# Moving GpSimd's barrier wait from behind the closing semaphore clear to ahead of it, in a row-sum kernel

## The chip, the cores and the metric

The kernel runs on one core of one Trainium2 chip. The metric is device time in microseconds; a kernel's time is the median of its executions. "The span" is the time from the first to the last recorded instruction of one profiled execution; the time holds some 1.78 us more than the span of the same execution (1.78 in both profiled kernels and all runs below but one). Engines are called VectorE (DVE), ScalarE (ACT), GpSimd (POOL), TensorE (PE) and SyncE (SP); a q behind such a name, as in POOLq or PEldq (TensorE), marks what the engine's sequencer runs itself. A transfer's landing is an update of its semaphore by the DMA; the last store has 16 of them, from 159.665 to 159.834 us in the kernel before, and counts as landed with the 16th (the clear that waits for it starts 24 ns later). The closing is the name here for what the trace holds behind the span's end: in the kernel before, 18 updates of one semaphore from 235 to 1902 ns behind it, and one or two of each of 246 others; the texts put it down to the runtime, which no trace shows. A wait is called met when its condition already holds as the engine comes to it.

## The reference

```python
def reference(x):            # x: 32 x 512 x 1024 float32
    return np.sum(x, axis=-1).astype(np.float32)
```

## The kernel before

The body streams x into SBUF in blocks of 16 rows per partition and sums rows on VectorE, with ScalarE helping at the end. It ends with a last store of 8 KB from SyncE. Behind the body stands a closing block that the framework writes: SyncE waits for what is outstanding, a first barrier of all engines, GpSimd's clear of the range of semaphores that the program used, and a second barrier. In a barrier the four other engines each run a drain that adds 1 to a "gather" semaphore, and then wait for a "release" semaphore; GpSimd waits until gather holds 4, takes 4 off, and adds 4 to release. An earlier change, already in the kernel before, lets the clear itself, not SyncE, wait for the landing of the last store:

```python
def wait_for_the_store_at_the_clear(nc):
    end = nc.main_func.blocks[-1]
    insts = list(end.instructions)
    # ... finds SyncE's last store and SyncE's drain ahead of the first barrier ...
    (wait,) = [w for w in info.on_wait if w.ant_name == stored]
    rest = [w for w in info.on_wait if w.ant_name != stored]
    insts[at] = copy.replace(
        insts[at], sync_info=mybir.SyncInfo(on_wait=rest, on_update=info.on_update)
    )
    clear = next(
        k
        for k, i in enumerate(insts)
        if i.engine == mybir.EngineType.Pool and isinstance(i, mybir.InstISA)
    )
    # ...
    insts[clear] = copy.replace(
        insts[clear], sync_info=mybir.SyncInfo(on_wait=[wait], on_update=[])
    )
    end.instructions = insts
```

As built, GpSimd's part of the closing block is, in order (gather and release stand for the barrier's two semaphores):

```
drain
wait gather >= 4, gather -= 4      first barrier
release += 4
drain
clear of the program's semaphores  waits for the last store's landing
drain
wait gather >= 4, gather -= 4      second barrier
release += 4
```

## Time and profile before

| | before |
|---|---|
| time, median of 3 (lowest to highest) | 161.72 us (161.71 to 161.91) |
| span of the profiled execution | 160.24 us, time of that execution 162.02 |
| DMA, mean over the span | 419 GB/s, 67.18 MB |
| last landing of the last store to the clear | 24 ns |
| clear's start to the span's end | 383 ns |

The first three rows say where the time goes: into the stream (the chain that ended last is DMA for 73% and VectorE for 25% of the span). The last two are what the change can touch. They come from the trace's records of single instructions and of semaphore updates, since the views round to 0.1 us. The lines of the views themselves are shown in the prediction. One further view of the kernel before, the DMA issues by line with KB each and us from issue to landing, shows the store that the clear waits for:

```profile
out_dram<-sums ACTq DMA_DIRECT2D x1, 56.0 KB, 2.1
out_dram<-sums SPq DMA_DIRECT2D x1, 8.0 KB, 1.4
```

The second line is the last store: 1.4 us from its issue at 158.41 us to its landing at 159.83, and inside those 1.4 us the first barrier ends (its last arrival is counted at 159.14) and all four arrivals of the second come in (the last at 159.46).

### The profile page before, as it was taken

What the parts mean: (1) busy time and instruction counts of PE and PEld (TensorE: products, weight loads), DVE (VectorE), ACT (ScalarE), POOL (GpSimd) and SP (SyncE); (2) the same over time, 40 slices, a digit from 0 to 9 for tenths busy, and PEclk for the clock granted to TensorE, in tenths of its full rate; (3) what the DMA queues carried; (4) which work ended last, traced back from release to release, by engine and by line L of the source; (5) the groups of instructions that cost most, each with busy time, mean ns of one, the idle gap of its engine ahead of it and who ended that gap; (6) DMA issues with size and microseconds to landing.
All of it is one profiled execution on the core that took longest, in us unless ns stands there. A gap on an engine that the chain in (4) does not pass through costs nothing.

```text
span 160.2 us, 125 instructions
## 1 busy us (share of the span) xinstructions
DVE 120.1 (75%) x22; ACT 17.3 (11%) x31; POOL 0.2 (0%) x4
## 2 busy tenths in 40 slices
DVE  0190059960799959999499994999949999497953
ACT  3000000000000000000000000000000000496953
POOL 0000000000000000000000000000000000000000
DMA  7999996996996996989969969969969969899994
GB/s 270 450 479 503 393 524 262 523 523 262 524 523 262 523 524 262 523 360 425 524 262 523 523 262 524 523 262 523 523 262 523 507 278 523 376 409 410 424 382 109
DMA packets 2928, 67.18 MB, mean 419 GB/s; under 512 B 1264, under 2 KB 1392, under 8 KB 1520
## 3 DMA queue, kind: packets, MB, share of 16 engines
q1 hardware_dynamic: 2016, 67.12, 97.7%
q10 hardware_dynamic: 912, 0.06, 0.3%
HBM read 67.11 MB, written 0.07 MB: 419 GB/s over the span
## 4 chain that ended last, share of the span: by engine, by line
DMA 73%; DVE 25%; SPq 1%; issue 0%; DVEq 0%
DMA t<-in_x_dram 73%; DVE sums L131 24%; SPq L170 1%; SPq L211 0%; DVE t L145 0%; DVEq L242 0%
## 5 line engine op out<-in xcount | busy, mean ns | idle before, releaser
L131 DVE TENSOR_REDUCE sums<-t 128x16 f32<-128x16384 f32 (+3 forms) x9 | 116.6, 12953 | 35.9 <-DMA t<-in_x_dram 35.9
L158 ACT ACTIVATE unread<-t 128x1024 f32<-128x1024 f32 x15 | 15.2, 1012 | 139.7 <-DMA t<-in_x_dram 139.7
L145 DVE CUSTOM_DVE_ANT_0 t<-t 128x512 f32<-128x512 f32 (+2 forms) x6 | 3.5, 602 | 2.4 <-DMA t<-in_x_dram 2.3
L158 ACT ACTIVATION_READ_ACCUMULATOR unread<-t 128x1 f32 x15 | 2.8, 187 | 0.0
L158 ACT ACT_TABLE_LOAD x1 | 1.3, 1283 | 0.8 <-PEq L231 0.8
L145 DVE DVE_READ_ACCUMULATOR2_ANT sums<- 128x1 f32 x5 | 0.4, 83 | 0.0
L231 POOL MEMSET const-bfloat16-1.0<- 128x1 bf16 x1 | 0.1, 101 | 0.0
L231 POOL MEMSET const-uint8-127<- 128x1 uint8 x1 | 0.1, 101 | 0.0
L231 POOL MEMSET const-float32-0.0<- 128x1 f32 x1 | 0.1, 98 | 0.2 <-issue 0.2
L231 POOL MEMSET const-float32-1.0<- 128x1 f32 x1 | 0.1, 98 | 0.0
L145 DVE DVE_READ_ACCUMULATOR2_ANT t<- 128x1 f32 x1 | 0.1, 83 | 0.0
L209 DVE MEMSET t<- 128x1 f32 x1 | 0.1, 59 | 0.0
## 6 DMA issues: line engine op xcount, KB each, us to landing
t<-in_x_dram SPq DMA_DIRECT2D x1, 6144.0 KB, 21.0
t<-in_x_dram SPq DMA_DIRECT2D x1, 4096.0 KB, 31.2
t<-in_x_dram SPq DMA_DIRECT2D x1, 2560.0 KB, 37.0
t<-in_x_dram SPq DMA_DIRECT2D x1, 2048.0 KB, 7.2
t<-in_x_dram SPq DMA_DIRECT2D x1, 1024.0 KB, 39.0
t<-in_x_dram SPq DMA_DIRECT2D x1, 280.0 KB, 39.2
t<-in_x_dram SPq DMA_DIRECT2D x1, 232.0 KB, 39.3
t<-in_x_dram SPq DMA_DIRECT2D x6, 41.1
```

The source lines that it names most:

```text
L131: return nc.vector.tensor_reduce(out=dst, in_=src, axis=mybir.AxisListType.X, op=mybir.AluOpType.add)
L145: return nc.vector.tensor_tensor_reduce(out=src[:, :n], in0=src[:, :n], in1=src[:, n:], scale=1.0, scalar=0.0, op0=mybir.AluOpType.add, op ...
L158: nc.scalar.activation(out=unread[:, :n], in_=src, func=mybir.ActivationFunctionType.Copy, accum_out=dst,)
L170: load = nc.sync.dma_start(out=block, in_=rows_from(j, n))
L209: nc.vector.memset(whole[:, width + 1 :], 0.0)
L231: nc = _bacc.Bacc("TRN2", target_bir_lowering=False, num_devices=1)
```

## The change

GpSimd's wait for the other engines at the second barrier goes ahead of the clear. It then falls into the time in which GpSimd waits for the store to land anyway (in the trace before, 369 ns from the last arrival at 159.465 to the landing at 159.834), and behind the clear only a drain stands ahead of the release. Nothing is added or dropped.

```diff
     insts[clear] = copy.replace(
         insts[clear], sync_info=mybir.SyncInfo(on_wait=[wait], on_update=[])
     )
+
+
+    at = next(
+        k
+        for k in range(clear + 1, len(insts))
+        if insts[k].engine == mybir.EngineType.Pool and isinstance(insts[k], mybir.InstEventSemaphore)
+    )
+    assert insts[at].sync_info.on_wait and "gather" in insts[at].sync_info.on_wait[0].ant_name
+    met = insts.pop(at)
+    insts.insert(clear, met)
     end.instructions = insts
```

## The prediction

From the recorded texts (this one and the expectation of after_again) passages are cut that told of the hardware what no run of this case shows; the cuts are marked. The sum here: one step of 79 ns off the span, 160.241 - 0.079 = 160.162 us, and with the 1.48 us outside the span 161.64 us. What the time outside the span consists of was not shown. "Here it is" stands for the part of the store's time behind its last packet, and "these" in rival B for the updates of the closing. That the cleared range does not hold the barrier's two semaphores shows in the trace before: those updated 21 to 65 ns behind the clear's start are 99 to 108, the barrier's are 96 and 97.

> **What bounds the kernel now.** I read the page first, part 1 and part 2, to see whether the change can touch what the kernel spends its time on.
>
> ```profile
> span 160.2 us, 125 instructions
> DVE 120.1 (75%) x22; ACT 17.3 (11%) x31; POOL 0.2 (0%) x4
> ...
> DMA  7999996996996996989969969969969969899994
> GB/s 270 450 479 503 393 524 262 523 523 262 524 523 262 523 524 262 523 360 425 524 262 523 523 262 524 523 262 523 523 262 523 507 278 523 376 409 410 424 382 109
> ```
>
> The DMA row stands at 6 to 9 tenths in every slice but the first and the last: the kernel is a stream of 67.11 MB from HBM, and VectorE (75% busy) follows it. GpSimd has 0.2 us of work in all. So the change is not in the stream. I then asked for busy time by stretches.
>
> ```profile
> core 0: us, DVE busy (x) ACT busy (x) POOL busy (x), PEclk, DMA share, GB/s
> 120.00:150.00 30.00, 26.80 (x3) 10.41 (x19) 0.00 (x0) 1.00 0.99 428
> 150.00:158.40 8.40, 5.94 (x14) 5.61 (x12) 0.00 (x0) 1.00 0.89 350
> 158.40:160.20 1.80, 0.00 (x0) 0.00 (x0) 0.00 (x0) 1.00 0.05 5
> ```
>
> The last row is the stage that the change edits: 1.80 us in which no engine does counted work and the DMA share is 0.05. It is 1.1% of the span. Even if the whole of it vanished the time would fall by less than 2%. The chain that ended last stops short of it, at the last sum:
>
> ```profile
> 24 pieces in order of time: start us, us, what
> ...
> 118.59 39.34 DMA t<-in_x_dram
> 157.93 0.05 issue
> 157.97 0.40 DVE t L145
> 158.38 0.01 DVEq L242
> ```
>
> So I went to the closing block itself: the view of the instructions that stand at the launch's line, limited to the window from 159.3 to 160.3 us.
>
> ```profile
> L242 ACTq EVENT_SEMAPHORE  x2: 17/17/17, 159.3 to 160.2; - x2
> L242 DVEq EVENT_SEMAPHORE  x2: 21/21/21, 159.3 to 160.2; - x2
> L242 PEldq EVENT_SEMAPHORE  x2: 51/51/51, 159.3 to 160.2; - x2
> L242 POOLq DRAIN  x2: 34/52/70, 159.3 to 160.0; - x2
> L242 POOLq EVENT_SEMAPHORE  x2: 17/17/17, 160.1 to 160.1; - x2
> ...
> L242 POOLq EVENT_SEMAPHORE_RANGE_CLEAR  x1: 93/93/93, 159.9 to 159.9; - x1
> ```
>
> Both semaphore instructions of GpSimd in this window stand behind the clear, at 160.1 us; the other engines are released at 160.2. One of the two is the wait that the change moves. The page rounds to 0.1 us, so the sizes below come from the trace's own records, in ns from the span's start, for the same instructions:
>
> ```
> 158412  SP store of the last 8 KB issued (348)
> 159240  first barrier: GpSimd's release
> 159321  GpSimd drain (70)
> 159373  SP, 159378 ACT, 159402 DVE, 159444 PE: drains of the second barrier
> 159465  last of the four arrivals counted on the gather semaphore
> 159464  last packet of the store ends
> 159834  16th landing of the store counted on its semaphore
> 159858  GpSimd clear of the semaphore range (93)
> 159980  GpSimd drain (34)
> 160058  GpSimd wait for the four arrivals (17)
> 160137  GpSimd release (17)
> 160178  SP, 160183 ACT, 160189 DVE, 160190 PE (51): released
> 160241  end of the span (PE's release instruction ends)
> ```
>
> The tail is one chain: store issue, landing at 159.834, clear 24 ns later, drain, gather wait, release, and the four releases. The four other engines had arrived at 159.465, some 370 ns before the store landed and almost 600 ns before GpSimd looks for them. The gather wait at 160.058 therefore waits for nothing; it costs only its own step.
>
> [...] the gather's record is 17 ns long, but the next instruction of GpSimd starts 79 ns after it (160058 to 160137), and the same pair in the first barrier is 78 ns apart (159162 to 159240). So 79 and not 17 ns is the cost of the step. [...] Here it is the 370 ns from the last packet's end (159464) to the last landing (159834): that wait is what the moved instruction can hide in.
>
> **The change part by part.** The diff takes GpSimd's wait for the gather semaphore (at least 4, then minus 4) from behind the drain that follows the clear and puts it ahead of the clear. Nothing is removed or added: listed engine by engine without waits and drains, the two programs differ in line numbers alone. In the built program the closing order on GpSimd becomes drain, gather wait, clear (still held for the store's landing), drain, release. The range that is cleared does not hold the barrier's own two semaphores, so nothing that the release needs is lost.
>
> (1) Removed from behind the landing: one step of 79 ns. The drain then hands over directly to the release. The drain's step to the next instruction was 78 ns (159980 to 160058), so the release should start at about 160.058 instead of 160.137: minus 79 ns on the path that sets the end.
>
> (2) Added ahead of the clear: the same step, met early. GpSimd's drain begins at 159.321 and its record ends at 159.391. The wait is then satisfied when PE's arrival is counted, 159.465, and starts about 159.49 (in the first barrier the wait started 24 ns after the last arrival, 159138 to 159162). One step of 78 ns later, about 159.57, GpSimd is at the clear, and the clear waits for the landing until 159.834. There is some 0.26 us of slack: cost on the path, zero.
>
> (3) Moved: the four releases follow the release by 41 to 53 ns as now, and PE's takes 51 ns. The clear, its drain and the store are as before. Sum: 160.241 - 0.079 = 160.162 us of span. The time holds 161.72 - 160.24 = 1.48 us more than the span of a profiled run[...]; the records of its barrier semaphore in the closing start at 160.476, 235 ns behind the span's end, and run on to 162.143. They follow the release and so should shift with it. So 161.72 - 0.08 = **161.64 us**, or 0.05% less.
>
> **The rivals.**
>
> A: the new wait ahead of the clear takes the store's place. If an engine came late to the second barrier, the clear would start late. For it: the arrivals of the second barrier can only follow the first barrier's release, 159.240, and PE took 204 ns from there. Against: an arrival would have to be 0.26 us later than it is. If it happened, the loss would be whatever exceeds the slack; the time would be at worst about as before, 161.7 to 161.8.
>
> B: the gain is swallowed behind the span. [...] If these were held by something other than the release (an engine that starts on its own clock, a fetch), the span would shrink by 79 ns and the time stay at 161.72. For it: the trace shows some 1.7 us of such updates and does not say what starts them. Against: every engine ends with the release, so none can enter earlier than that. I give this a fifth.
>
> C: the clear, or the drain behind it, changes length once the release stands directly behind. A drain of GpSimd took 34 here, 70 and 41 ns in its other two places, and 179 in the opening. A change by 36 ns would leave the time at 161.6 to 161.7. The step of 78 behind the drain is the same as the step behind a gather, which suggests a fixed cost of the sequencer rather than one of that pair.
>
> D: the DMA stream drowns it. The three times before are 161.71, 161.72 and 161.91: a spread of 0.20 us, more than twice the gain. The stream of 67 MB runs for 158 us and the change does not touch it, so any difference over 0.1 us either way would be the stream's noise and not the change.
>
> **Range and chances.** The middle is 161.64. The range is one spread of the three times, 0.20 us, to each side: rounded, 161.45 to 161.85. For faster by over 2% the time would have to fall below 158.5, that is by 3.2 us, nearly the whole of the 1.80 us tail and the 1.48 us outside the span together; for slower by over 2% it would have to exceed 164.95, which only a missed barrier could do. So within 2%: 0.99, and half a percent each way for what I have not seen.
>
> **What the profile will show.** Right on (1): behind the clear stand a drain and one semaphore instruction of GpSimd, and from the clear's start to the span's end the trace has 0.30 us instead of 0.38 (159858 to 160241). Right on (2): the moved wait starts near 159.5 in this trace's terms, before the landing, and the clear still starts some 24 ns behind the landing. Wrong by A: the clear starts later than that behind the landing. Wrong by B: clear to span's end shrinks, but the time against interleaved runs of the kernel before does not. Wrong by C: the drain behind the clear is longer than 34 ns or its step longer than 78. The span itself may differ by 0.1 to 0.2 us from the stream alone, so these distances from the landing decide and not the span. What would make the number wrong is a stream that runs differently on that day or chip.

## The result, and the profile after

| | before | after |
|---|---|---|
| time, median of 6 executions each, in the same rounds | 161.81 us (161.68 to 162.12) | 161.70 us (161.40 to 162.03) |
| ratio, 95% interval | | 0.9993 (0.9975 to 1.0011) |
| span of the profiled execution | 160.241 us | 159.625 us |
| last landing of the store | 159.834 us | 159.312 us |
| landing to the clear's start | 24 ns | 24 ns |
| clear's start to the span's end | 383 ns | 289 ns |
| span's end to the reported time | 1.78 us | 1.78 us |

A ratio is the mean time of one kernel's fast runs over the mean of the other's of the same rounds, so it is not quite the ratio of the medians in the first row. The two kernels are the same within 2%, and the timing alone does not even show a direction: the interval holds 1. The two profiled spans differ by 616 ns, but 522 of these lie ahead of the store's landing (159.834 - 159.312), in the stream that the change does not touch. The other 94 are the change.

The head and part 1 of the page of the kernel after, span and busy time:

```profile
span 159.6 us, 125 instructions
...
DVE 120.1 (75%) x22; ACT 17.3 (11%) x31; POOL 0.2 (0%) x4
```

The same instructions, the same busy time. The stretches, taken so that the last one begins about when the store is issued, as in the prediction:

```profile
core 0: us, DVE busy (x) ACT busy (x) POOL busy (x), PEclk, DMA share, GB/s
120.00:150.00 30.00, 26.84 (x3) 10.93 (x21) 0.00 (x0) 1.00 1.01 434
150.00:157.80 7.80, 5.36 (x14) 5.10 (x10) 0.00 (x0) 1.00 0.91 353
157.80:159.60 1.80, 0.06 (x2) 0.00 (x0) 0.00 (x0) 1.00 0.06 5
```

The last row is as wide as before because the stretch was taken so; in it the DMA share is 0.06, and the only counted work is 0.06 us of the last sum. The end of the chain that ended last:

```profile
118.20 39.23 DMA t<-in_x_dram
157.43 0.02 issue
157.45 0.40 DVE t L155
157.85 0.01 DVEq L252
```

It ends with the same two pieces, 0.53 us earlier than before, behind the same DMA wait, and this chain does not go on to the store or the closing block in either kernel. So neither view can judge this change. The closing block's instructions in the window from 158.78 to 159.70 us can (the columns: duration in ns as lowest, median and highest, then first and last start in us):

```profile
L252 POOLq DRAIN  x2: 34/52/70, 158.8 to 159.5; - x2
L252 POOLq EVENT_SEMAPHORE  x2: 17/17/17, 159.0 to 159.5; - x2
...
L252 PEldq DRAIN  x1: 8/8/8, 158.9 to 158.9; - x1
L252 POOLq EVENT_SEMAPHORE_RANGE_CLEAR  x1: 93/93/93, 159.3 to 159.3; - x1
```

Before, both of GpSimd's semaphore instructions in such a window read 160.1, behind the clear at 159.9. Now the first stands at 159.0, ahead of the clear at 159.3, and only the release is behind it at 159.5. The records of the kernel after, in ns from the span's start, give the sizes:

```
158716  first barrier: GpSimd's release
158920  PE: drain of the second barrier (the last of the four)
158941  last of the four arrivals counted on the gather semaphore
158965  GpSimd wait for the four arrivals (17), moved
159312  16th landing of the store counted on its semaphore
159336  GpSimd clear (93)
159458  GpSimd drain (34)
159521  GpSimd release (17)
159574  PE (51): released
159625  end of the span
```

Against the prediction's list: the wait starts 24 ns behind the last arrival, the clear still 24 ns behind the landing, so the move costs nothing in its new place. Behind the drain the release now follows in 63 ns, where the wait took 78 and the release 79 more: 157 - 63 = 94.

### The profile page after: what moved, and what is told of

Read it like the earlier page. It is cut to its first block, busy times and chain, and to the rows that moved or that the text cites. A ratio compares the mean times of both kernels' runs of the same rounds, so it can differ in the third digit from the quotient of the medians.

```text
span 159.6 us, 125 instructions
## 1 busy us (share of the span) xinstructions
DVE 120.1 (75%) x22; ACT 17.3 (11%) x31; POOL 0.2 (0%) x4
## 4 chain that ended last, share of the span: by engine, by line
DMA 73%; DVE 25%; SPq 1%; issue 0%; DVEq 0%
DMA t<-in_x_dram 73%; DVE sums L141 24%; SPq L180 1%; SPq L221 0%; DVE t L155 0%; DVEq L252 0%
```

## The experiments

Twelve kernels ran, each profiled; three were timed in rounds. All gave correct results. For a single execution of a one-core kernel the state (fast or slow) is unknown, so nothing below is read from such times alone; distances inside one trace are used. In this table all are in ns, from the records:

| run | landing to clear | clear to span's end | landing to reported time |
|---|---|---|---|
| before (profiled) | 24 | 383 | 2186 |
| after (profiled) | 24 | 289 | 2088 |
| after_again | 23 | 291 | 2099 |
| late_before | 24 | 383 | 2185 |
| late_after | 229 | 289 | 2301 |
| atsp_before | 493 | 382 | 2662 |
| atsp_after | 643 | 289 | 2712 |
| pad20_behind | 24 | 1605 | 3408 |
| release_first | 23 | 93 | 1949 |
| steps | 24 | 2089 | 3891 |
| update_behind | 24 | 368 | 2173 |
| wait_behind | 25 | 352 | 2159 |
| no_drain | 25 | 226 | 2034 |
| no_drain_before | 24 | 319 | 2124 |

The last column has the reported time of the profiled execution, given to 10 ns, less the landing. Edits that add instructions use one helper; `idle` is a wait for the release semaphore to be 0, which is met where it is used:

```python
def pad(at, like, waits=(), updates=()):
    pads.append(f"I-{9000 + len(pads)}")
    info = mybir.SyncInfo(on_wait=list(waits), on_update=list(updates))
    insts.insert(at, copy.replace(like, name=pads[-1], sync_info=info))
```

### Is the moved wait hidden, and by how much? (late_before, late_after)

The theory: the wait is free ahead of the clear because the landing comes later than the arrivals, with 0.26 us of slack. The rival: its place behind or ahead of the clear is all that counts. Both kernels get a TensorE that arrives late at the second barrier:

```diff
+    second = places(E.PE, mybir.InstDrain)[-1]
+    for _ in range(4):
+        pad(second, insts[places(E.PE, EV)[0]], waits=idle)
```

> The kernel before, with four waits that are already met put ahead of TensorE's drain of the second barrier, so that TensorE arrives late, by an estimated 0.3 to 0.5 us (some 80 to 120 ns each; TensorE's records are 51 ns). Theory (the wait for the arrivals stands behind the clear and finds them long there, by almost 0.6 us): nothing moves; the clear starts 24 ns after the store's last landing, as before, and from the clear's start to the span's end it is 383 ns. Rival (a late arrival costs wherever the wait stands): the clear to the end grows by 0.3 us or more.

> The changed kernel with the same late TensorE. Theory (the moved wait hides in the store's landing, with 0.27 us of slack and no more): the clear starts late, 24 ns plus the delay less 0.27 us behind the landing, so some 50 to 250 ns instead of 24; from the clear to the end it stays 289 ns; the gain of 94 ns is given back wholly or in part. Rival (the wait ahead of the clear is free whatever the arrival): 24 ns and 289 ns.

The closing block of late_before, and then that of late_after, each from its first release on:

```profile
L260 PEldq EVENT_SEMAPHORE  x6: 51/51/51, 159.0 to 159.9; - x6
...
L260 POOLq EVENT_SEMAPHORE_RANGE_CLEAR  x1: 93/93/93, 159.6 to 159.6; - x1
L260 PEldq DRAIN  x1: 8/8/8, 159.6 to 159.6; - x1
```

```profile
L270 PEldq EVENT_SEMAPHORE  x6: 51/51/51, 159.6 to 160.6; - x6
...
L270 PEldq DRAIN  x1: 8/8/8, 160.2 to 160.2; - x1
L270 POOLq EVENT_SEMAPHORE_RANGE_CLEAR  x1: 93/93/93, 160.4 to 160.4; - x1
```

In the first fence TensorE's drain, its arrival, is at 159.6 like the clear, and the clear did not care: the records have it 54 ns behind the clear's start, and the clear 24 ns behind the landing. In the second fence the clear stands 0.2 us behind TensorE's arrival, and the landing was at 160.139: the clear waited for TensorE. The four pads made TensorE some 469 ns later than in the kernel after (673 against 204 ns behind the first release), and the clear came 205 ns later behind the landing (229 - 24), so the slack was 264 ns in this execution, as the prediction had it. With this TensorE the kernel after is 111 ns worse from landing to span's end (229 + 289 = 518, against 24 + 383 = 407). The rival is out.

### What if there is nothing to hide in? (atsp_before, atsp_after)

The earlier change is undone in both kernels: SyncE waits for the store ahead of the first barrier, and the clear waits for nothing of its own.

```diff
-    rest = [w for w in info.on_wait if w.ant_name != stored]
-    insts[at] = copy.replace(
-        insts[at], sync_info=mybir.SyncInfo(on_wait=rest, on_update=info.on_update)
-    )
...
-    insts[clear] = copy.replace(
-        insts[clear], sync_info=mybir.SyncInfo(on_wait=[wait], on_update=[])
-    )
```

> The kernel before with SyncE waiting for the store ahead of the first barrier, and the clear waiting for nothing of its own: the landing no longer lies between the second barrier's arrivals and the clear. Theory: from GpSimd's first release to the clear some 190 ns (81 to the drain, then its 70 to 120), from the clear to the end 383 as before, so some 570 ns from the first release to the span's end.

> The changed kernel with the same edit, so that the moved wait has nothing to hide in. Theory (the move pays only because the landing covers it): the clear waits for TensorE's arrival, some 330 ns behind the first release (249 to the gather wait, 78 on), then 289 to the end: about 615 ns from the first release to the end, 40 ns slower than the same kernel without the move. Rival (a step less behind the clear is 94 ns won in any case): about 480 ns.

From GpSimd's first release, the clear started after 180 ns without the move and after 330 with it, and the span ended after 562 and 619 ns. From the landing it is 493 + 382 = 875 against 643 + 289 = 932 ns. So the same move loses 57 ns here (the expectation had some 40), although the part behind the clear is 93 ns shorter as always. The closing block of atsp_after shows why:

```profile
L243 POOLq EVENT_SEMAPHORE  x3: 17/17/17, 160.0 to 160.5; - x3
...
L243 PEldq DRAIN  x1: 8/8/8, 160.2 to 160.2; - x1
L243 POOLq EVENT_SEMAPHORE_RANGE_CLEAR  x1: 93/93/93, 160.3 to 160.3; - x1
```

The clear stands behind TensorE's arrival at 160.2, for which it now waits; without the move (atsp_before) it began 24 ns ahead of TensorE's drain. In these runs the move paid only where another wait covered it.

### Does the time follow the tail? (after_again, pad20_behind)

The rival B of the prediction was that the runtime's closing, behind the span, swallows what the tail gains. One run repeats the change in more rounds; the other makes the tail longer by twenty met waits behind the clear of the kernel before:

```diff
+    wait_on_gather = insts[places(E.Pool, EV)[0]]
+    behind = places(E.Pool, mybir.InstISA)[-1] + 1
+    for _ in range(20):
+        pad(behind, wait_on_gather, waits=idle)
```

> The changed kernel itself, in five rounds beside the kernel before. Theory: the span's tail is 94 ns shorter and the time follows, ratio 0.9994, 161.6 to 162.3 us [...], with an interval of about 0.001 to each side that will most likely still hold 1. Rival (the runtime's closing swallows it): ratio 1.0000. The time alone will hardly tell these apart; the tail in the profile must again be 24 ns from landing to clear and 289 ns from clear to the span's end.

> The kernel before with twenty waits that are already met put directly behind the clear on GpSimd. Theory (a step of GpSimd behind the clear costs its full 78 ns, and the time follows the release): clear to end 383 + 20 x 78 = about 1.94 us, the time longer by about 1.57 us, ratio 1.0097. Rival (the runtime's closing is held by something other than the release, and swallows tail time): the time grows by clearly less than the span's tail.

after_again: 161.77 us against 161.97 (medians, fast runs), ratio 0.9990, interval 0.9971 to 1.0008. As expected, the time does not settle it; the tail was 23 and 291 ns.

pad20_behind: 162.90 us, ratio 1.0057, interval 1.0039 to 1.0075, so slower clear of the noise, though within 2%. The tail is 1605 ns, 1222 longer and not 1560: a met wait behind a met wait costs 61 ns a step, so the expectation (78) missed the size of a step. GpSimd's part of its closing block from the clear on:

```profile
L261 POOLq EVENT_SEMAPHORE  x22: 17/17/17, 159.8 to 161.1; - x22
L261 POOLq EVENT_SEMAPHORE_RANGE_CLEAR  x1: 93/93/93, 159.6 to 159.6; - x1
L261 POOLq DRAIN  x1: 34/34/34, 161.0 to 161.0; - x1
```

The 22 are the twenty pads, the gather wait and the release. For the question asked, the profiled execution is exact where the rounds are not: from the landing to the reported time it has 3408 ns against 2186, which is 1222 more, all of the tail's growth. (In the rounds 1222 ns would be a ratio of 1.0075, the upper end of the interval.) In every run of the table but one the reported time lies 1.78 us behind the span's end, within 10 ns. In these runs the closing swallows nothing as long as the release ends the span.

### What does the step consist of? (steps, update_behind, wait_behind, no_drain, no_drain_before)

The prediction had 79 ns for the step, the trace 94. A train of 26 small steps between the drain and the release of the kernel after measures each pair by the starts of its records (W a met wait, U an update, T an update that takes four back, D a drain):

```diff
+    for step in "WWWWUUUUTDDDDWDWDUDUDUDUDT":
+        at = places(E.Pool, EV)[-1]
+        if step == "D":
+            pad(at, free_drain)
+        else:
+            pad(at, gather, idle if step == "W" else (), {"U": give, "T": take}.get(step, ()))
```

> The changed kernel with a train of 26 small steps on GpSimd between the drain behind the clear and the release: four met waits, four updates, one taking back, four drains, then waits and drains and updates and drains by turns. It measures what each step costs by the starts of its records. Theory (a met wait itself adds some 15 ns to the step of the instruction that carries it, because the release behind a drain came 63 ns after it and the wait behind the same drain 78): wait behind wait 78, update behind update about 63, wait behind drain 78, update behind drain 63. Rival (the 15 ns belong to the pair drain and wait alone): update behind update 78, as wait behind wait.

| from, to | ns from start to start |
|---|---|
| wait, wait | 61 (the first pair 65) |
| wait, update | 43 |
| update, update | 78 to 79 |
| update, drain | 81 |
| wait (behind a drain), drain | 50 to 51 |
| drain, drain | 60 to 61 |
| drain, wait | 78 to 79 |
| drain, update | 63 to 64 |

None of the four pairs came out as forecast, and half of the theory fell. A met wait does add to its own instruction's step: 15 ns behind a drain (78 - 63), 18 behind a wait (61 - 43). But an update behind an update takes 78, not 63, because an update delays what follows it: by 35 ns ahead of an update (78 - 43), by some 30 to 35 ahead of a drain (81 - 51, or 81 - 46 with the last of the twenty waits of pad20_behind, which stands behind other waits). An instruction of this kind that carries neither would thus cost 43 ns, an estimate from these pairs. The moved instruction carries both: 43 + 15 + 35 = 93. Two kernels put one half of it back behind the drain of the kernel after:

```diff
+    info = insts[met].sync_info                                    # update_behind
+    pad(release, insts[met], updates=info.on_update)
+    insts[met] = copy.replace(
+        insts[met], sync_info=mybir.SyncInfo(on_wait=info.on_wait, on_update=[])
+    )
```

```diff
+    pad(release, insts[met], waits=idle)                           # wait_behind
```

> The moved instruction split: its wait stays ahead of the clear, its update (minus 4) stands alone behind the drain, where the kernel before has both. Theory, from the train of steps (an instruction of this kind 43 ns, some 15 to 18 more if it carries a met wait, some 35 more if it carries an update): it costs 78 of the 94 ns, so the clear to the end is 289 + 78 = 367 ns. Rival (it is the waiting that costs, as my prediction had it with 79 for the wait): well under that, near 289 + 15.

> The other half: wait and update ahead of the clear as in the changed kernel, and behind the drain one instruction that only waits, for something already met. Theory of the sum: 15 for the wait plus 43 for the instruction, 58 ns, so the clear to the end is 347 ns. Rival (wait and update cost alike): 289 + 79 = 368.

The update alone costs 79 ns (368 - 289), its rival's 15 is out. The wait alone costs 63 (352 - 289), 5 more than the sum of the pairs had it; the rival's 79 is out. The records have these 5 elsewhere too: a wait that stands directly behind a drain or the clear hands over some 5 ns later than one behind another wait (65 or 66 against 61 to a wait, 48 against 43 to an update, 50 to 51 against 46 to a drain). Of the moved instruction, then, the update that takes the four arrivals off is dearer than the wait that has long been met. Last, the drain behind the clear is dropped, from the kernel after and from the kernel before:

```diff
+    clear = places(E.Pool, mybir.InstISA)[-1]
+    drain = places(E.Pool, mybir.InstDrain)[-1]
+    assert drain > clear
+    insts.pop(drain)
```

> The changed kernel without the drain between the clear and the release. Theory: the release starts some 122 ns behind the clear's start, where the drain started, so the clear to the end is 289 - 63 = 226 ns.

> The kernel before without the same drain. Theory (the saving belongs to the moved instruction and not to its pairing with the drain): the wait starts about 136 ns behind the clear, the release 79 later, the clear to the end about 319 ns, so the move is again worth some 94 ns against the changed kernel without the drain. Rival (15 of the 94 belong to the pair of drain and wait): the difference between the two kernels without the drain is about 79.

226 and 319 ns, as expected to the nanosecond. The move is worth 93 ns here too, so its size does not hang on the drain, and the drain itself costs another 63 or 64. The some 15 ns of a wait show here without any drain: from the clear's start to the next start it is 137 ns where that carries a wait and 121 where it does not.

### A version that goes further (release_first)

The release can go ahead of the clear as well. The other engines then leave the program while GpSimd still waits for the store, and the clear is the program's last instruction. GpSimd alone has to hold the end until the store has landed, and the first barrier has already shown that nobody still waits on the cleared semaphores (in the trace before, the last such wait of another engine, SyncE's, starts at 159.074 us, and the first barrier's last arrival is counted at 159.138).

```diff
+    at = places(E.Pool, EV)[-1]          # the release
+    release = insts.pop(at)
+    insts.insert(clear, release)
+    ...                                  # and the drain behind the clear is dropped, as in no_drain
```

> The changed kernel with GpSimd's release put ahead of the clear as well, and the drain behind the clear dropped: the clear is then the last instruction of the program. Theory: the other engines are released some 0.2 us before the landing, and the span ends with the clear, 24 + 93 = 117 ns behind the landing, where the changed kernel has 313 and the kernel before 407: 290 ns less than before, and the time follows by 0.2 to 0.3 us, ratio about 0.9982. Rival (the runtime's closing is held otherwise): span shorter, time as before, ratio 1.0000.

161.40 us against 161.97 (medians), ratio 0.9970, interval 0.9952 to 0.9989: faster than the kernel before beyond the noise, though by far less than 2%. The records give its true size. In its closing block the releases of the other engines stand ahead of the clear:

```profile
L269 POOLq EVENT_SEMAPHORE  x2: 17/17/17, 158.9 to 159.0; - x2
...
L269 PEldq EVENT_SEMAPHORE  x1: 51/51/51, 159.0 to 159.0; - x1
L269 POOLq EVENT_SEMAPHORE_RANGE_CLEAR  x1: 93/93/93, 159.3 to 159.3; - x1
```

From the landing to the span's end it is 23 + 93 = 116 ns, against 407 before: 291 less. From the landing to the reported time it is 1949 against 2186: 237 less. So here, and only here, some 54 ns of the span's gain are lost behind the span (the reported time lies 1.83 us behind its end). The ratio's middle, 0.49 us (0.3% of 162), is no evidence of a larger gain: 0.24 us would be a ratio of 0.9985, inside the interval.

The records of the semaphore with 18 updates in the closing tell where the 54 ns may arise. In the kernel before its first three updates come 235, 269 and 474 ns behind the span's end, which is TensorE's. In release_first the first two again come 235 and 269 ns behind TensorE's last instruction, which now lies ahead of the span's end, and the third 527 ns behind the span's end. By the steps measured above, GpSimd can go on 79 ns behind the start of a release and 122 behind the start of the clear; from there to the third update it is 499 ns in the kernel before and 498 here. So the third update seems to follow GpSimd, which is free 25 ns ahead of the span's end in the kernel before and 29 ns behind it here: 25 + 29 = 54. This is an estimate from two traces; no run varied it.

## Why the prediction was right

**The bound.** The prediction held that the stream bounds the kernel and that the tail is the only stage touched. The result confirms it: the time is the same within the noise, and 522 of the 616 ns between the two profiled spans lie ahead of the store's landing. (One slip of reading: in the DMA row the first slice, 7 tenths, is no exception to "6 to 9"; only the last is.)

**Step (1), the step taken from behind the landing,** was right in mechanism and small by 15 ns: 94 instead of 79. The failed term is "The drain's step to the next instruction was 78 ns", read as a property of the drain that would stay when the wait is gone. Behind the same drain the release comes after 63 ns. The missing 15 belonged to the wait carried by the next instruction. The train of steps shows the same 63 and 78 side by side, and rival C's argument, that an equal 78 behind a drain and behind a gather "suggests a fixed cost of the sequencer", is refuted by it: one 78 is 63 and a wait, the other 43 and an update. Rival C itself came true with the other sign: the drain's record stayed at 34 ns, but its step grew shorter by 15, not longer.

**Step (2), the slack,** was right: 0.26 us predicted, 264 ns from late_after. That the two agree so closely is in part luck. The prediction took 78 ns from the moved wait to the clear; late_after has 96, and 81 where the clear carries no wait (atsp_after). It also counted the slack to the landing and not to the clear's start 24 ns later, and these two errors nearly cancel. Rival A is real, but needs a later arrival: a TensorE 469 ns late turned the gain of 94 into a loss of 111, and by the slack some 360 ns (264 + 94, an estimate) would use the gain up. So the prediction's "at worst about as before" for rival A was too mild.

**Step (3) and rival B.** The tail moved as a whole, and the closing followed it to within 10 ns, shown by pad20_behind with 1222 ns in both. The prediction's "1.48 us more than the span of a profiled run" took the median of three other executions less the span of a profiled one; the profiled execution itself took 162.02 us, and the right difference is 1.78. The slip cancels in the predicted time, which only subtracts the gain from the median.

**Rival D and the number.** The predicted 161.64 us and the measured median of 161.70 agree, but that is not evidence for the mechanism: the kernel before itself read 161.72 in its first three executions, 161.81 in six, and 161.97 in eleven beside the later runs.

**The records.** A semaphore instruction's record did not show its waiting or its update: GpSimd's records of 17 ns stand for steps of 43 to 81 ns in the train, and 96 to the clear in late_after. In the kernel after, the moved wait's record starts only 24 ns behind the last arrival, though the drain ahead of it ended 98 ns earlier (158.867), and the release's update is counted 25 ns behind its start, 8 ns behind its record's end. A met wait added 15 to 18 ns to a step.

**What stays open.** Why a met wait costs 15 ns in one pair and 18 in another, and why one behind a drain hands over 5 ns later than one behind a wait, no run here tells. That the closing waits for GpSimd in release_first is an estimate from the records and was not tested.

## What to carry to other kernels

A barrier's bookkeeping (waits that are long met, updates, drains) cost 61 to 94 ns an instruction on GpSimd here, though its records show 17 or 34, and the four met waits on TensorE cost 469 ns together; put what does not depend on the last transfer ahead of the wait for it, but check the slack, since the same move without cover lost 57 ns here. For a change of this size compare distances from a common event inside single traces, here the store's landing, since the times scatter by several times the gain (0.44 us over six executions of the kernel before, against 94 ns). And when a step is timed from start to start, ask which of its two instructions owns the gap before subtracting it.

## Sizes that the traces gave

- Wait and update lay outside the 17 ns of a semaphore instruction's record (in the kernel after 24 ns from the last arrival to the moved wait's start, 8 ns from the release's end to its update). On GpSimd in the train of steps: 43 ns from a met wait to an update, 15 to 18 more where the later one waits, 30 to 35 more where the earlier one updates, 60 to 61 from drain to drain.
- For the last store of the kernel before (issued by SyncE, 8 KB) 840 ns passed from the issue's start to the first packet (158.412 to 159.252), 212 in packets, and 370 from the last packet to the landing (159.464 to 159.834): most of it lies ahead of the data.
- The reported time ended 1.78 us behind the last engine's release in every kernel but one, and 1.83 us behind the clear in release_first, where the other engines were released early. In the kernel before, the records of the closing's semaphore run from 0.235 to 1.902 us behind the span's end.
